# An earlier gate for casting loads, slice-wise accumulation over four tiles, and three matmuls moved ahead of a wait

## The chip, the core and the metric

The kernel runs on one core of a Trainium2 chip. The metric is the time of one execution on the device in microseconds (us), the median of several runs. A core has a tensor engine (PE, with its weight loads as PEld), a vector engine (DVE), a scalar engine (ACT), GpSimd (POOL) and a sync engine (SP), which run side by side and wait for each other by semaphores. Its transfers run on 16 DMA engines. Here the sync engine issues plain loads and stores, and GpSimd issues loads that cast float32 to bf16 on the way.

## The reference

Two matrix products with a gelu between them; a is 1024x1024, b 1024x2048, c 2048x1024, all float32.

```python
def reference(a, b, c):
    h = np.matmul(a, b)
    h = 0.5 * h * (1 + np.tanh(np.sqrt(2 / np.pi) * (h + 0.044715 * h ** 3)))
    return np.matmul(h, c).astype(np.float32)
```

## The kernel before

The kernel works in bf16, and in three stages. The first multiplies a with the left half of b (columns 0 to 1023), 16 output tiles of 128x512, by plain accumulation over eight slices k of the contraction. The second does the right half of b, the third the product with c, both with a scheme of seven block products instead of eight (`Seven`). The change touches the first stage only.

In that stage the first half of the contraction (k = 0 to 3) comes as float32 by eight plain loads of 512 KB each, which ACT and DVE cast to bf16. The second half (k = 4 to 7), the rest of b, and c come by casting loads from GpSimd. GpSimd issues none of them before it has copied one element of a plain load into `gate`: that copy waits for the load.

```python
    def load_a(h, q):        # rows 512*h.., columns 256*q.. of a, as float32
        nc.sync.dma_start(out=sta[:, h, q], in_=av[:, 4 * h:4 * h + 4, ds(q * 256, 256)])

    def load_b(q, c):        # slices k = 2q, 2q+1 of b, columns 512*c..
        nc.sync.dma_start(out=stb[:, c, 2 * q:2 * q + 2], in_=bv[:, 2 * q:2 * q + 2, ts(c, H)])

    load_a(0, 0)             # 1
    load_b(0, 0)             # 2
    load_a(1, 0)             # 3
    load_a(0, 1)             # 4
    load_b(1, 0)             # 5
    load_a(1, 1)             # 6
    load_b(0, 1)             # 7
    load_b(1, 1)             # 8

    nc.gpsimd.tensor_copy(gate, sta[:, 1, 1, 3, 0:1])
    # ... the casting loads, all on GpSimd's queue, in this order:
    for h in (0, 1):
        for m in (0, 2):     # a, second half of the contraction: four of 256 KB (as bf16)
            st = pieces("m", 4, [128, 2, H], BF16, "a2")
            nc.gpsimd.dma_start(out=st, in_=av[:, 4 * h + m:4 * h + m + 2, ds(KH * 128, H)])
            a2[h, m] = st
    for k in range(KH, KT):  # b, left half, k = 4..7: four of 256 KB
        nc.gpsimd.dma_start(out=b1[:, k], in_=bv[:, k, 0:1024])
    # ... four of 512 KB for the right half of b, eight of 512 KB for c
```

The tensor engine takes a tile of the output in a PSUM bank and adds one slice at a time; `turn1` and `turn` transpose pieces of a with the identity matrix (eight transposes), and DVE copies the result to `aT`.

```python
    def mm1(p, t, h, ks, k0=0, k1=KT):
        for k in ks:
            nc.tensor.matmul(p, b1[:, k, ts(t, 128)], aT[:, h, k],
                             start=(k == k0), stop=(k == k1 - 1))

    def block(h, tiles, ks):
        for k in ks:
            for t in tiles:
                mm1(ps[h, t], t, h, (k,), 0, KH)

    # ...
    block(0, range(4), (0, 1))
    turn1(1, 0, 5, cast_a(1, 0, nc.vector))
    turn1(0, 1, 7, cast_a(0, 1, nc.scalar))
    for t in range(3):
        ps[1, t] = bank(4 + t)
    block(1, range(3), (0, 1))
    cast_b(2, 0)
    cast_b(3, 0)
    ab = cast_a(1, 1, nc.vector)
    block(0, range(4), (2,))
    turn1(1, 1, 7, ab)
    block(0, range(4), (3,))
    for k in range(KH):
        cast_b(k, 1)         # ACT casts loads 7 and 8
    # ...
    for t in range(4):
        leave(0, t)          # ACT (even t) and DVE (odd t) move banks to SBUF
    block(1, range(3), (2, 3))
    ps[1, 3] = bank(7)
    mm1(ps[1, 3], 3, 1, range(KH), 0, KH)
    for t in range(4):
        leave(1, t)
    # ...
    T2 = [(h, t) for h in range(2) for t in range(4, 8)]
    for n, (h, t) in enumerate(T2[:7]):       # first half of the contraction
        ps[h, t] = bank(n)
        mm1(ps[h, t], t, h, range(KH))
        if n in (2, 3, 4, 5):
            turn(n // 4, 2 * (n % 2), 7)
    one.t3()
    one.t2()
    for h, t in T2[:7]:                       # second half
        mm1(ps[h, t], t, h, range(KH, KT))
        gelu(t, h, ps[h, t])
    p = bank(7)
    mm1(p, 7, 1, range(KT))
    gelu(7, 1, p)
    # ... then the tiles moved out above, second half: banks 0 to 7 once more
```

Of the kernel before, what the change touches and what calls it, by code (L numbers as in the profile page):

```python
# [19 lines left out]
def kernel(ctx, tc, a, b, c, out):  # L20
    nc = tc.nc
# [4 lines left out]
    KT = K // 128  # L26
# [13 lines left out]
    def slot(tag, shape, dt, name):  # L40
        return big.tile(shape, dt, name=name, tag=tag)

    def bank(i, shape=(128, H), dt=F32, name="ps"):
        return pp.tile(list(shape), dt, name=name, tag=f"bank{i}", padded_shape=None)

    def pieces(tag, bufs, shape, dt, name):
        return small.tile(shape, dt, name=name, tag=tag, bufs=bufs)
# [5 lines left out]
    gate = consts.tile([128, 1], F32, name="gate")  # L53
# [9 lines left out]
    KH = KT // 2  # L63
    stb = slot("x0", [128, 2, KH, H], F32, "stb")
    sta = slot("x1", [128, 2, 2, 4, 256], F32, "sta")
# [13 lines left out]
    load_b(0, 1)  # L79
    load_b(1, 1)  # L80

    nc.gpsimd.tensor_copy(gate, sta[:, 1, 1, 3, 0:1])  # L82
    nc.scalar.activation(g, warm[:, 0:1], AF.Gelu_apprx_tanh)
    wps = bank(7, name="warmps")
    for _ in range(7):
# [18 lines left out]
    def copy(eng, dst, src):  # L104
        if eng is nc.scalar:
            nc.scalar.activation(dst, src, AF.Copy)
        else:
            nc.vector.tensor_copy(dst, src)
# [6 lines that stand above are left out]
    def gelu(t, h, p):  # L115
        nc.scalar.activation(hT[h][:, t], p, AF.Gelu_apprx_tanh)  # L116

    ps = {(0, t): bank(t) for t in range(4)}
# [7 lines left out]
    def cast_a(h, q, eng):  # L126
        ab = pieces("ab", 2, [128, 4, 256], BF16, "ab")
        copy(eng, ab, sta[:, h, q])
        return ab

    def turn1(h, q, i, ab):
        pt = bank(i, (128, 2, H), BF16, "pt")
        for n in range(2):
            for m in range(4):
                nc.tensor.transpose(pt[:, n, ts(m, 128)], ab[:, m, ts(n, 128)], ident)
        nc.vector.tensor_copy(aT[:, h, 2 * q:2 * q + 2], pt)

    def cast_b(k, c, n=1):
        for i in range(n):
            r = ds(i * (H // n), H // n)  # L140
            nc.scalar.activation(b1[:, k, ds(c * H + i * (H // n), H // n)], stb[:, c, k, r], AF.Copy)  # L141
# [5 lines that stand above are left out]
# [5 lines left out]
    cast_b(1, 0)  # L152
    block(0, range(4), (0, 1))
    turn1(1, 0, 5, cast_a(1, 0, nc.vector))
    turn1(0, 1, 7, cast_a(0, 1, nc.scalar))
    for t in range(3):
        ps[1, t] = bank(4 + t)
    block(1, range(3), (0, 1))
    cast_b(2, 0)
    cast_b(3, 0)  # L160
    ab = cast_a(1, 1, nc.vector)
# [88 lines left out]
    T2 = [(h, t) for h in range(2) for t in range(4, 8)]  # L250
# [4 lines left out]
            turn(n // 4, 2 * (n % 2), 7)  # L255
    one.t3()
    one.t2()
    for h, t in T2[:7]:
        mm1(ps[h, t], t, h, range(KH, KT))
        gelu(t, h, ps[h, t])  # L260
    p = bank(7)
    mm1(p, 7, 1, range(KT))
# [3 lines left out]
    for n in range(8):  # L266
        h, t = divmod(n, 4)
# [156 lines left out]
```

## Time and profile before

| | |
|---|---|
| time, median of 3 runs | 122.31 us (122.23 to 122.33) |
| span of the profiled execution | 120.5 us |
| PE busy | 112.4 us, 93% |
| DVE, ACT, POOL busy | 88.4, 53.3, 14.6 us |
| loads landing: first, sixth, eighth plain load | 4.5, 12.6, 15.3 us |
| granted clock of PE | 0.993 |

Times in the profile count from the start of the span. A line of the timeline names the start, the length, the engine, the line of the kernel (L112 is the matmul in `mm1`, L135 the transposes of `turn1`, L108 and L106 copies and casts on DVE and ACT, L141 ACT's casts of b, L82 the gate), and in brackets how long the engine had been idle and what ended that. A busy matmul is drawn with its way through the array, so it overlaps the next one; how fast a stream runs is read from the starts. The landing times above are those at which the first reader of a load began.

### The profile page before, as it was taken

Reading aid. Unit: us, or ns where it says so; the run is one execution under the profiler, and the core shown is the slowest. Engines: PE = TensorE matmul, PEld = TensorE weight load, DVE = VectorE, ACT = ScalarE, POOL = GpSimd, SP = SyncE. Lnnn points to the kernel's source line nnn. Section 1 sums busy time; section 2 is a strip of 40 time slices with the busy share of each in tenths; the row PEclk is TensorE's granted clock in tenths of the full one; section 3 lists DMA queues with packets and bytes.
Section 4 is the critical chain, followed back from the end, with each engine's and each line's share of the span. In section 5 each row is a group of like instructions: output and inputs, shape, how many; then the busy total and the mean of one; then the engine's idle time right before and its main releaser. Section 6 shows DMA issues by size and latency. Waiting matters only on the chain.

```text
span 120.5 us, 1459 instructions
## 1 busy us (share of the span) xinstructions
PE 112.4 (93%) x550; PEld 72.7 (60%) x550; DVE 88.4 (73%) x92; ACT 53.3 (44%) x86; POOL 14.6 (12%) x27
## 2 busy tenths in 40 slices
PE   6985999969999999999999999999999999999970
PEld 2633545624444444888888444468888888888850
DVE  0243589488017899978779999979999996892490
ACT  4046490005637779946669636900012595100000
POOL 2000895462322000000000000000000000000000
PEclk9999999999999999999999999999999999999997
DMA  2999999999999999997000000062000002004695
GB/s 85 283 371 367 305 167 202 168 205 207 207 207 213 212 212 209 212 212 145 1 5 0 5 0 0 0 250 98 0 0 0 5 0 87 0 0 174 235 352 197
DMA packets 11463, 16.86 MB, mean 140 GB/s; under 512 B 705, under 2 KB 5825, under 8 KB 11457
## 3 DMA queue, kind: packets, MB, share of 16 engines
q0 software_dynamic: 5952, 8.39, 40.1%
q1 hardware_dynamic: 5504, 8.39, 19.8%
q8 instruction: 4, 0.07, 0.2%
q14 instruction: 3, 0.02, 0.1%
HBM read 20.97 MB, written 4.19 MB: 209 GB/s over the span
## 4 chain that ended last, share of the span: by engine, by line
PE 62%; DMA 21%; DVE 6%; POOL 4%; SPq 2%; issue 1%; ACT 1%; DVEq 0%; ACTq 0%
PE ps L239 50%; PE ps L112 12%; DMA b<-in_b_dram 8%; DMA sta<-in_a_dram 8%; DMA out_dram<-ot 5%; DVE x L197 4%; POOL a L93 2%; DVE ot L285 2%; POOL b L96 1%; SPq L68 1%; SPq L71 1%; DVE ot L370 1%; ACT u L280 1%; POOL gate L82 0%; DVEq L285 0%
## 5 line engine op out<-in xcount | busy, mean ns | idle before, releaser
L112 PE MATMUL ps<-aT,b 128*128 128x512 bf16 x128 | 29.2, 379 | 1.7 <-DMA b<-in_b_dram 1.2
L239 PE MATMUL ps<-x,s 128*128 128x512 f32 x128 | 29.6, 391 | 0.0
L239 PEld LDWEIGHTS ps<-x,s 128*128 128x128 f32 x128 | 24.0, 188 | 5.1
L112 PEld LDWEIGHTS <-b 128*128 128x128 bf16 x128 | 12.1, 98 | 15.9 <-DMA b<-in_b_dram 2.0
L239 PE MATMUL ps<-x,x 128*128 128x512 f32 x64 | 14.8, 389 | 0.0
L239 PE MATMUL ps<-c_sb,hT 128*128 128x512 bf16 x64 | 14.0, 379 | 0.0
L239 PEld LDWEIGHTS ps<-x,x 128*128 128x128 f32 x64 | 12.0, 188 | 2.5
L280 ACT ACTIVATE v<-ps 128x512 f32<-128x512 f32 x8 | 4.8, 599 | 17.1 <-PE ps L239 17.1
L116 ACT ACTIVATE hT<-ps 128x512 bf16<-128x512 f32 x12 | 6.8, 595 | 12.1 <-PE ps L112 12.1
L239 PE MATMUL ps<-x 128*128 128x512 f32 x48 | 11.3, 393 | 0.0
L239 PEld LDWEIGHTS <-hT 128*128 128x128 bf16 x64 | 6.2, 97 | 7.6 <-issue 0.3
L270 DVE TENSOR_TENSOR half<-ps,half 128x512 f32<-128x512 f32 x8 | 5.5, 692 | 7.0 <-PE ps L112 6.6
L239 PEld LDWEIGHTS ps<-x 128*128 128x128 f32 x48 | 9.0, 188 | 2.0
L197 DVE TENSOR_TENSOR x<-c_sb 128x1024 fp32r<-128x1024 bf16 x8 | 9.2, 1215 | 0.0
L285 DVE TENSOR_TENSOR ot<-ps,v 128x512 f32<-128x512 f32 x8 | 5.3, 687 | 4.6 <-DMA out_dram<-ot 3.8
L141 ACT ACTIVATE b<-stb 128x512 bf16<-128x512 f32 (+1 forms) x9 | 4.7, 573 | 6.6 <-DMA stb<-in_b_dram 6.6
L285 DVE TENSOR_TENSOR ot<-ps,u 128x512 f32<-128x512 f32 x8 | 5.4, 691 | 3.0 <-ACT u L280 3.0
L116 ACT ACTIVATE hT<-ot 128x512 bf16<-128x512 f32 x12 | 7.0, 624 | 1.2 <-DVE ot L285 1.2
L239 PE MATMUL ps<-aT,b 128*128 128x512 bf16 x32 | 7.1, 379 | 0.0
L102 POOL DMA_DIRECT2D c_sb<-in_c_dram x8 | 5.7, 712 | 8.9 <-DMA b<-in_b_dram 8.9
L280 ACT ACTIVATE p<-ps 128x512 f32<-128x512 f32 x8 | 4.6, 594 | 4.8 <-PE ps L239 4.8
L116 ACT ACTIVATE hT<-half 128x512 bf16<-128x512 f32 x8 | 5.0, 631 | 2.6 <-DVE half L270 2.6
(47 smaller groups left out, 114.7 us busy)
## 6 DMA issues: line engine op xcount, KB each, us to landing
c_sb<-in_c_dram POOLq DMA_DIRECT2D x8, 512.0 KB, 20.2
out_dram<-ot SPq DMA_DIRECT2D x16, 256.0 KB, 2.1
sta<-in_a_dram SPq DMA_DIRECT2D x4, 512.0 KB, 6.9
stb<-in_b_dram SPq DMA_DIRECT2D x4, 512.0 KB, 8.9
b<-in_b_dram POOLq DMA_DIRECT2D x4, 512.0 KB, 13.8
a<-in_a_dram POOLq DMA_DIRECT2D x4, 256.0 KB, 5.6
b<-in_b_dram POOLq DMA_DIRECT2D x4, 256.0 KB, 8.9
```

Source lines behind the costliest of these rows:

```text
L68: nc.sync.dma_start(out=sta[:, h, q], in_=av[:, 4 * h:4 * h + 4, ds(q * 256, 256)])
L71: nc.sync.dma_start(out=stb[:, c, 2 * q:2 * q + 2], in_=bv[:, 2 * q:2 * q + 2, ts(c, H)])
L93: nc.gpsimd.dma_start(out=st, in_=av[:, 4 * h + m:4 * h + m + 2, ds(KH * 128, H)])
L102: nc.gpsimd.dma_start(out=c_sb[:, t:t + 2], in_=cv[:, t:t + 2])
L112: nc.tensor.matmul(p, b1[:, k, ts(t, 128)], aT[:, h, k], start=(k == k0), stop=(k == k1 - 1))
L116: nc.scalar.activation(hT[h][:, t], p, AF.Gelu_apprx_tanh)
L141: nc.scalar.activation(b1[:, k, ds(c * H + i * (H // n), H // n)], stb[:, c, k, r], AF.Copy)
L197: nc.vector.tensor_tensor(out=dst[:, r], in0=x[:, r], in1=y[:, r], op=op)
L239: nc.tensor.matmul(p[:, ds(c0, w)], l[:, k, ts(j, 128)], r[:, k, ds(c0, w)], start=(start and k == 0), stop=(k == self.kt - 1), skip_group ...
L270: nc.vector.tensor_tensor(out=half[:, h, t], in0=p, in1=half[:, h, t], op=ADD)
L280: nc.scalar.activation(st, p, AF.Copy)
L285: nc.vector.tensor_tensor(out=ot, in0=p, in1=st, op=ADD)
```

## The change

It has three parts, all in the first stage. The gate copies an element of the fifth plain load instead of the sixth, so that GpSimd issues the casting loads earlier. Three of the six matmuls of the block for the lower rows of a (slice k = 0) are put ahead of the transposes of the fourth plain load, to stand where the tensor engine waits for that load's cast. And the second half of the contraction over the first four of the tiles in `T2` goes slice by slice over all four, instead of tile by tile, so that a slice of b is needed later than before. Nothing is computed otherwise, and the number of instructions is the same.

```diff
-    nc.gpsimd.tensor_copy(gate, sta[:, 1, 1, 3, 0:1])
+    nc.gpsimd.tensor_copy(gate, stb[:, 0, 3, 0:1])
...
     turn1(1, 0, 5, cast_a(1, 0, nc.vector))
-    turn1(0, 1, 7, cast_a(0, 1, nc.scalar))
     for t in range(3):
         ps[1, t] = bank(4 + t)
-    block(1, range(3), (0, 1))
+    ab = cast_a(0, 1, nc.scalar)
+    block(1, range(3), (0,))
+    turn1(0, 1, 7, ab)
+    block(1, range(3), (1,))
...
-    for h, t in T2[:7]:
-        mm1(ps[h, t], t, h, range(KH, KT))
+    for k in range(KH, KT):
+        for h, t in T2[:4]:
+            mm1(ps[h, t], t, h, (k,))
+    for n, (h, t) in enumerate(T2[:7]):
+        if n >= 4:
+            mm1(ps[h, t], t, h, range(KH, KT))
         gelu(t, h, ps[h, t])
```

## The prediction

> **What bounds the kernel now.** I read the page first, then the chain that ended last, the waits, the timeline up to 48 us, and short windows for the DMA traffic. From the page's third and fourth parts and the chain in order of time (start us, length us, what):
>
> ```profile
> PE 62%; DMA 21%; DVE 6%; POOL 4%; SPq 2%; issue 1%; ACT 1%; DVEq 0%; ACTq 0%
> ```
>
> ```profile
> 3.48 9.11 DMA sta<-in_a_dram
> ...
> 12.64 0.18 POOL gate L82
> 12.82 2.92 POOL a L93 x4
> 15.74 1.57 POOL b L96 x3
> 17.32 9.97 DMA b<-in_b_dram
> ...
> 27.33 14.20 PE ps L112 x65
> 41.53 60.69 PE ps L239 x272
> ```
>
> From 27.33 us on the tensor engine decides. I looked for starts of its matmuls over 0.3 us apart after that time and found only two (0.42 us each, at 48 and 80 us). So whatever moves the 27.33 moves the end, one for one. Before 27.33 the chain runs through the gate: the sixth load lands, GpSimd opens the gate, issues eight casting loads, and the last slice of b (k=7) ends a wait of the tensor engine. The chain looks as if an earlier gate would pay in full. Two other views say that it can't.
>
> The timeline (start us, length us, engine, line, operation, idle before):
>
> ```profile
> 9.00 0.62 PE L135 MATMUL pt<-ident,ab 128*128 128x128 bf16 x8
> ...
> 10.93 0.62 PE L135 MATMUL pt<-ident,ab 128*128 128x128 bf16 x8 [1.31 <-ACT ab L106]
> ...
> 12.68 0.69 DVE L108 CAST ab<-sta 128x1024 bf16<-128x1024 f32 x1 [0.40 <-DMA sta<-in_a_dram]
> ...
> 13.99 5.85 PE L112 MATMUL ps<-aT,b 128*128 128x512 bf16 x26
> ...
> 15.27 1.15 ACT L141 ACTIVATE b<-stb 128x512 bf16<-128x512 f32 x2 [0.15 <-DMA stb<-in_b_dram]
> ...
> 16.32 2.04 ACT L106 ACTIVATE half<-ps 128x512 f32<-128x512 f32 x4
> ```
>
> ```profile
> 24.30 1.46 PE L112 MATMUL ps<-aT,b 128*128 128x512 bf16 x6
> ...
> 26.09 0.39 PE L112 MATMUL ps<-aT,b 128*128 128x512 bf16 x1 [0.34 <-DMA b<-in_b_dram]
> ...
> 27.33 14.20 PE L112 MATMUL ps<-aT,b 128*128 128x512 bf16 x65 [0.85 <-DMA b<-in_b_dram]
> ```
>
> One matmul of 512 columns takes (14.20-0.38)/64 = 0.216 us from start to start. The six at 24.30 are four of tile 6 and k=4, k=5 of the first tile; that tile's k=6 and k=7 then wait for their slices. Without waits k=7 would have started at 24.30+7x0.216 = 25.81; it started at 27.33. So **1.52 us** is really lost, more than the 1.2 us in the table of waits, since a busy matmul is drawn 0.38 us long.
>
> The windows of one microsecond (the last three columns are clock, DMA share, GB/s):
>
> ```profile
> 13.00:14.00 1.00, 1.00 (x13) 0.64 (x11) 0.38 (x1) 0.04 (x1) 1.00 (x2) 1.00 1.04 383
> 14.00:15.00 1.00, 1.00 (x8) 0.45 (x6) 0.80 (x2) 1.00 (x2) 1.00 (x2) 1.00 0.88 156
> 15.00:16.00 1.00, 1.00 (x6) 0.42 (x5) 1.00 (x2) 0.85 (x3) 1.00 (x3) 1.00 1.06 135
> ```
>
> The eight plain loads run the DMA engines full until 14. The casting loads replace them: the trace's packets by queue have the first casting packet at 14.43, 1.8 us after the gate's copy at 12.64, and the plain queue's last data at 14.8. The rate is counted in bytes written, half of those read where a load casts, so about 207 (28 to 31 us) is a casting load's full rate; at 15 to 16 the queue is still starting.
>
> **What the Trainium skill says.** "DMA: Bandwidth & Descriptors", section "Queues, rings and completion order", says that each DMA engine round-robins between the queues it has work for. So two queues that both have work share, and neither is free for the other. This trace shows almost no overlap of the two (14.4 to 14.8), so it neither confirms nor denies it. The same page, "Latency and other measured facts", gives about 1 us to the first byte on the GpSimd path; here it was 1.8 us from the gate's copy, of which the first issue is 0.74. "TensorE: Matmul & The Clock Gate", section "Back-to-back issue gap", gives some 216 ns for an isolated 512-column matmul and 131 in a stream; here 216 is the spacing in the stream too, and 131 is not reached. "PSUM — Partial Sum Buffer", section "The four PSUM rules", lets accumulation groups in different banks interleave, since a group's start clears its own bank only; so going slice by slice costs no extra instruction. The trace of before has it in the first block (four banks, k outermost) at the same 0.216 us.
>
> **The change part by part.** No instruction is added or removed.
>
> *Slice by slice.* With k outermost over four tiles, k=4 of four tiles comes first (0.86 us), then k=5, and so on: k=6 is needed 8x0.216 = 1.73 us after the start of this part, k=7 2.59 us after it. The part starts at 24.30+4x0.216 = 25.16, so they are needed at 26.89 and 27.75. They landed at 26.09 and 27.33. Even with unchanged landings both waits go, with 0.4 us to spare: **-1.52 us**. The four gelus then come together; ScalarE needs 0.60 each, 2.4 us, against 12 matmuls of tiles 4 to 6 (2.6 us) and the eight of the last tile before the first bank is used again. No new wait.
>
> *Three matmuls ahead.* The tensor engine waits from 9.6 to 10.93 for ScalarE's cast of the fourth piece of a. Three matmuls of tile row 1 (0.65 us) now stand there: they need the transposed piece that VectorE finished copying at 10.35, so they run 10.4 to 11.05, and the transposes start some 0.1 us later than now. That removes 0.65 us of work from after the wait, but the next stop swallows it: the transposes at 13.55 need VectorE's cast of the sixth load, 12.68+0.69 = 13.37, which landed at 12.6 either way. They can come from 13.55 to 13.43 and no further: **-0.12 us**.
>
> *The gate.* It waits for the fifth load, not the sixth. ScalarE's cast of that load (the trace's timeline has it at 11.13) puts its landing near 11.1, so the gate opens some 1.5 us sooner, at 11.15, and casting packets start at about 14.43-1.5 = 12.95. The sixth load's data is through by then (12.07 in the packets). The seventh has half a microsecond left, the eighth all of its 1.35: the plain queue has about 1.4 us of work left (mean over the 16 engines), of which 1.25 after the slower first casting packets. From there it shares. If the shares are equal, each 2 KB plain packet (2048 B x16/385 GB/s = 85 ns) is followed by a casting packet (1024 B x16/207 GB/s = 79 ns), and the last plain load comes 1.25x79/85 = 1.2 us later. If the casting queue starts as slowly as it did (25, 59, 72 packets in the first half microseconds against a steady 100), some 135 of them come in between: 135/16x79 ns = 0.7 us. I take **d = 1.0**.
>
> Who waits for the eighth load? ScalarE casts it at 15.27, in two (1.15 us), then moves the first bank out (0.58, from 16.32 to 16.90); the first of the 12 matmuls on the right half of b waits for both. It started at 17.09 (13.99+14x0.216, and 0.08 of a hiccup), so there was 0.13 us of slack on ScalarE's side after the semaphore. With the 0.12 of the reordering the tensor engine would come there at 16.97, just when ScalarE is done. So all of d becomes a new wait on the tensor engine: **+d = +1.0 us**. What the earlier gate brings in return, k=4 to k=7 perhaps 0.5 us sooner, is worth nothing, since slice by slice they are in time anyway.
>
> Sum: -1.52 - 0.12 + 1.0 = -0.64 us, and 122.31 - 0.64 = 121.67. I put it a little lower, **121.6 us**, since the slow start of the casting queue is what the trace shows, and equal shares are what it doesn't.
>
> **The rivals.** (1) Plain loads undisturbed: if the casting queue gets nothing while the other has work, d is 0 and the time 120.7. For it: the plain packets at 14.5 to 14.7, beside the first casting ones, took 84 to 95 ns as ever, while those casting packets took 350 to 1000. Against it: that is the tail of the queue, some 20 packets. (2) The starved plain load: the casting queue gets half or more from its first packet, and its reads are slower than steady (130 ns a packet at 15 us against 98 later). Then d is 1.6 to 2, the wait removed comes back as a wait for ScalarE's cast, and the time is 122.3 to 122.7. For it: queues share. (3) The gate pays as the chain suggests: k=7 lands 1.5 us sooner and everything follows. Against it: DMA share is about 1 from 3 us to 54 us, so the work only changes order; only the 0.3 us of idle engines and the slow start around 14.5 can be won. (4) A new wait for k=7 because the casting loads come no sooner while the tensor engine does: the 0.4 us to spare speak against it.
>
> **Range and chances.** d between 0.3 and 1.7 gives 121.0 to 122.4; I take 120.9 to 122.3. Even d = 0 is -1.3%, so faster by over 2% would need a gain that no step has; slower by 2% would need d above 4 us.
>
> **What would show it.** The table of waits of after should have no wait of the tensor engine for b's casting loads, and a new one of 0.7 to 1.2 us, near 17 us, for ScalarE's casts or its moves of the first banks; ScalarE should wait for the last stb load until 16 to 16.5 instead of 15.27. The gate's copy should stand at 11.1 to 11.2. The wait of the transposes for ScalarE's cast should shrink from 1.31 to near zero, and the transposes of the sixth load should start at 13.43. The steady part (65 matmuls at 27.33) should start 0.6 us sooner in equal count. If the eighth load still lands at 15.3, rival 1 holds; if it lands after 16.9, rival 2.

## The result, and the profile after

| | before | changed |
|---|---|---|
| median | 122.32 us (4 runs, 122.23 to 122.36) | 120.73 us (4 runs, 120.46 to 122.70) |
| ratio | | 0.9861, interval 0.9844 to 0.9878 |

By the medians the change takes off 1.59 us, 1.3%; by the ratio it is 1.7 us (1.5 to 1.9). The prediction was 121.6 with a range from 120.9 to 122.3, so the kernel is faster than its range. Its rival 1 (plain loads undisturbed) had named 120.7.

One of the four runs, at 122.70 us, was a slow one, in whose trace the tensor engine ran at half pace from 8 to 11 us; the ratio leaves it out, and the profile read here is that of the same kernel measured again (120.68 us). In this kernel the matmul of stage 1 is still L112 and the transposes of the first half L135; the second stage's matmul is L241, since lines moved by two.

The timeline of the changed kernel (start, length, engine, line, operation, idle before), to be laid beside the lines shown of before:

```profile
10.36 0.81 PE L112 MATMUL ps<-aT,b 128*128 128x512 bf16 x3 [0.78 <-DVE aT L136]
...
11.18 0.18 POOL L82 COPY gate<-stb 128x1 f32<-128x1 f32 x1 [9.87 <-DMA stb<-in_b_dram]
...
12.70 0.69 DVE L108 CAST ab<-sta 128x1024 bf16<-128x1024 f32 x1 [0.35 <-DMA sta<-in_a_dram]
...
13.45 0.62 PE L135 MATMUL pt<-ident,ab 128*128 128x128 bf16 x8
...
13.91 5.85 PE L112 MATMUL ps<-aT,b 128*128 128x512 bf16 x26
...
15.29 1.15 ACT L141 ACTIVATE b<-stb 128x512 bf16<-128x512 f32 x2 [0.16 <-DMA stb<-in_b_dram]
16.35 2.04 ACT L106 ACTIVATE half<-ps 128x512 f32<-128x512 f32 x4
...
24.21 4.48 PE L112 MATMUL ps<-aT,b 128*128 128x512 bf16 x19
```

The gate's copy stands at 11.18 instead of 12.64, so GpSimd does issue 1.46 us sooner. But the eighth plain load is read at 15.29, against 15.27 before: nothing was taken from it. The 26 matmuls begin at 13.91 instead of 13.99 and go on without a hole. From 24.21 on there is no stop for a slice of b, where before there were two, at 26.09 and 27.33. The chain shows what that is worth at the end; the second stage starts at 39.91 us instead of 41.53, 1.62 us sooner:

```profile
24.37 3.24 PE ps L112 x15
...
27.66 10.74 PE ps L112 x49
...
38.45 1.46 PE ps L112 x6
39.91 25.31 PE ps L241 x113
```

In the table of waits (waiter, releaser, us in total, times, longest) between 4 and 30 us the tensor engine's matmuls and transposes have these three, and none for a load:

```profile
PE ps L112 <- ACT b L141: 1.0, 1, 1.0
PE ps L112 <- DVE aT L136: 0.8, 1, 0.8
...
PE pt L135 <- DVE ab L108: 0.2, 1, 0.2
```

And the windows of one microsecond, with the clock, the DMA share and GB/s in the last three columns:

```profile
13.00:14.00 1.00, 0.97 (x11) 0.55 (x10) 0.39 (x1) 0.02 (x1) 1.00 (x2) 1.00 1.05 387
14.00:15.00 1.00, 1.00 (x7) 0.40 (x5) 0.89 (x2) 1.00 (x2) 1.00 (x3) 1.00 1.18 262
15.00:16.00 1.00, 1.00 (x6) 0.46 (x5) 1.00 (x2) 0.84 (x3) 1.00 (x3) 1.00 1.24 204
```

From 13 to 14 the plain loads still have their full rate, 387 GB/s, though the first casting load was issued by 12.13 (11.30, where the issue begins, and 0.83 for it). From 15 the casting loads are at full rate at once (204 against 135 before). So the earlier gate put them in line sooner, and they went when most of the plain loads were through.

### The profile page after: what moved, and what is told of

It is laid out like the page before. It is cut to its first block, busy times and chain, and to the rows that moved or that the text cites. A ratio compares the mean times of both kernels' runs of the same rounds, so it can differ in the third digit from the quotient of the medians.

```text
span 120.9 us, 1452 instructions
## 1 busy us (share of the span) xinstructions
PE 112.8 (93%) x544; PEld 72.6 (60%) x550; DVE 88.5 (73%) x92; ACT 52.8 (44%) x86; POOL 14.7 (12%) x27
## 4 chain that ended last, share of the span: by engine, by line
PE 77%; DMA 10%; DVE 7%; issue 1%; ACT 1%; SPq 0%; DVEq 0%; ACTq 0%
PE ps L241 50%; PE ps L112 24%; DMA out_dram<-ot 5%; DMA stb<-in_b_dram 5%; DVE x L199 4%; DVE ot L291 2%; PE pt L187 2%; DVE aT L136 1%; PE pt L135 1%; DVE ot L376 1%; ACT u L286 1%; SPq L68 0%; ACT b L141 0%; DVEq L291 0%; DVEq L376 0%
## 5 line engine op out<-in xcount | busy, mean ns | idle before, releaser
L112 PE MATMUL ps<-aT,b 128*128 128x512 bf16 x124 | 30.5, 395 | 2.9 <-ACT b L141 1.7
L241 PE MATMUL ps<-x,s 128*128 128x512 f32 x128 | 29.6, 391 | 0.0
L241 PEld LDWEIGHTS ps<-x,s 128*128 128x128 f32 x128 | 24.0, 188 | 5.1
L112 PEld LDWEIGHTS <-b 128*128 128x128 bf16 x128 | 12.5, 100 | 17.4 <-issue 2.9
L241 PE MATMUL ps<-x,x 128*128 128x512 f32 x64 | 14.8, 389 | 0.0
L241 PE MATMUL ps<-c_sb,hT 128*128 128x512 bf16 x62 | 13.9, 379 | 0.1
L241 PEld LDWEIGHTS ps<-x,x 128*128 128x128 f32 x64 | 12.0, 188 | 2.5
L116 ACT ACTIVATE hT<-ps 128x512 bf16<-128x512 f32 x12 | 6.3, 602 | 12.4 <-PE ps L112 12.4
L241 PE MATMUL ps<-x 128*128 128x512 f32 x48 | 11.3, 394 | 0.0
L241 PEld LDWEIGHTS <-hT 128*128 128x128 bf16 x64 | 6.2, 98 | 7.6 <-issue 0.3
L241 PEld LDWEIGHTS ps<-x 128*128 128x128 f32 x48 | 9.0, 188 | 2.0
L241 PE MATMUL ps<-aT,b 128*128 128x512 bf16 x32 | 7.1, 379 | 0.0
L136 DVE COPY aT<-pt 128x1024 bf16<-128x1024 bf16 x4 | 2.8, 692 | 5.1 <-PE pt L135 5.1
```

Of the source, the lines that this page charges most:

```text
L112: nc.tensor.matmul(p, b1[:, k, ts(t, 128)], aT[:, h, k], start=(k == k0), stop=(k == k1 - 1))
L241: nc.tensor.matmul(p[:, ds(c0, w)], l[:, k, ts(j, 128)], r[:, k, ds(c0, w)], start=(start and k == 0), stop=(k == self.kt - 1), skip_group ...
```

## The experiments

Each kernel was timed beside the kernel before on the same chip, whose median was 122.4 to 122.5 us. A time is the median of four runs or more, except where one run is named. "Landing", "read at" and the first packets are those of one trace of each kernel.

**The changed kernel once more**, for the trace shown above; the kernel is the same.

> The changed kernel once more, for a trace whose tensor clock is full: 120.5 to 120.8 us. Theory A (plain loads undisturbed: while the plain queue has work the casting queue takes next to nothing from it): the eighth plain load is read by ScalarE at 15.2 to 15.4 us, as before, and no wait of the tensor engine at 17 us. Theory B (the queues do share, but the casting queue starts some 2 us after its gate and slowly, so it meets only the plain queue's tail): the eighth load at 15.4 to 15.8. Theory C (the load is late by my 1 us, and something else made up for it): 16 us or later.

Measured: 120.82 us, ScalarE reads the eighth load at 15.29, and the twelve matmuls on the right half of b run without a wait. Theory C falls. The 15.29 is in A's range, but it does not tell A's rule from a late start as in B, since the first casting packet came only at 14.00, 2.8 us after the gate's copy.

**The gate back at the sixth load, the rest of the change kept.**

```diff
-    nc.gpsimd.tensor_copy(gate, stb[:, 0, 3, 0:1])
+    nc.gpsimd.tensor_copy(gate, sta[:, 1, 1, 3, 0:1])
```

> The changed kernel with the gate back at the sixth load. If the slices alone take the waits away, as the prediction has it (k=6 needed at 26.9, k=7 at 27.7, landed at 26.1 and 27.3): 120.7 us, the same as the changed kernel within 0.2 us, under theories A and B. Under theory C it is faster than the changed kernel by up to 1 us. If the gate is what brought the gain: 121.5 or more, with waits for the casting loads of b on the tensor engine.

Measured: 120.70 us (120.53 to 120.86), beside 120.82 (120.51 to 121.72) with the gate at the fifth load on the same chip. In the changed kernel no gain from the earlier gate shows within this spread.

**The slices alone**, and **the three matmuls alone**, each in the kernel before.

```diff
-    for h, t in T2[:7]:
-        mm1(ps[h, t], t, h, range(KH, KT))
+    for k in range(KH, KT):
+        for h, t in T2[:4]:
+            mm1(ps[h, t], t, h, (k,))
+    for n, (h, t) in enumerate(T2[:7]):
+        if n >= 4:
+            mm1(ps[h, t], t, h, range(KH, KT))
         gelu(t, h, ps[h, t])
```

> The kernel before with the slices alone. The prediction's step: both waits for k=6 and k=7 go, 1.52 us less, 120.8 us, and no wait of the tensor engine for the casting loads of b. If the gain needs the earlier gate: 121.3 us or more and a wait left. The spread between chips and runs is 0.2 us.

Measured: 120.83 us, ratio 0.9864 (0.9850 to 0.9879). That is 1.7 us, the whole of the change within the interval (1.5 to 1.8 us). The timeline of this kernel has 20 matmuls in one piece, and GpSimd's issue that waits for the k=7 slice at 27.33 (in the kernel before such an issue, at 27.57, follows 0.24 us after the matmul on that slice); the tensor engine doesn't need that slice before 24.17+16x0.216 = 27.62:

```profile
24.17 4.70 PE L112 MATMUL ps<-aT,b 128*128 128x512 bf16 x20
...
27.33 0.72 POOL L102 DMA_DIRECT2D c_sb<-in_c_dram  x1 [0.52 <-DMA b<-in_b_dram]
```

```diff
-    turn1(0, 1, 7, cast_a(0, 1, nc.scalar))
     for t in range(3):
         ps[1, t] = bank(4 + t)
-    block(1, range(3), (0, 1))
+    ab = cast_a(0, 1, nc.scalar)
+    block(1, range(3), (0,))
+    turn1(0, 1, 7, ab)
+    block(1, range(3), (1,))
```

> The kernel before with the three matmuls moved alone. The prediction's step: 0.12 us before the transposes of the sixth load, and then nothing at the end, because the wait for k=7 stays where its load puts it: 122.3 us, within 0.2 us of the kernel before. If the order matters by itself: 121.7 or less.

Measured: 122.37 us, ratio 0.9990 (0.9981 to 0.9998), so 0.12 us (0.02 to 0.23). The waits for the slices are all still there, and a little longer than before: in this trace the tensor engine arrives 0.07 us sooner (24.23), and the k=7 slice lands 0.22 us later:

```profile
26.23 0.39 PE L112 MATMUL ps<-aT,b 128*128 128x512 bf16 x1 [0.55 <-DMA b<-in_b_dram]
...
27.55 1.25 PE L112 MATMUL ps<-aT,b 128*128 128x512 bf16 x5 [0.93 <-DMA b<-in_b_dram]
```

**The gate at the fifth load alone**, in the kernel before.

```diff
-    nc.gpsimd.tensor_copy(gate, sta[:, 1, 1, 3, 0:1])
+    nc.gpsimd.tensor_copy(gate, stb[:, 0, 3, 0:1])
```

> The kernel before with the gate at the fifth load alone. The tensor engine still wants k=6 and k=7 at 25.6 and 25.8 us. If they land 0.3 to 0.5 us sooner, as the prediction has it, 121.8 to 122.0 us; if they land 1.5 us sooner, as the chain of the kernel before suggests, 120.8 to 121.0 us; with the eighth load late by 1 us, 122.3 or more. Theory A and B: between 121.0 and 122.0 us.

Measured: 121.32 us, by the medians 1.1 us less than the kernel before; the ratio is uncertain (0.9851, 0.9782 to 0.9920). In the trace the k=6 wait is gone, and k=7 starts at 26.41 instead of 27.33, 0.92 us sooner:

```profile
24.36 1.67 PE L112 MATMUL ps<-aT,b 128*128 128x512 bf16 x7
...
26.41 2.33 PE L112 MATMUL ps<-aT,b 128*128 128x512 bf16 x9 [0.37 <-DMA b<-in_b_dram]
```

Without waits k=7 would have started at 24.36+7x0.216 = 25.87, so 0.54 of the 1.52 us lost before remain. By medians and trace the earlier gate is worth about 1 us where nothing else removes the waits, and nothing that shows where the slices do. The gains of the two parts overlap; they don't add up.

**The gate at the third, the first, and the fourth load**, in the changed kernel: how much do the plain loads suffer from casting loads that are issued in the middle of them?

```diff
-    nc.gpsimd.tensor_copy(gate, stb[:, 0, 3, 0:1])
+    nc.gpsimd.tensor_copy(gate, sta[:, 1, 0, 3, 0:1])   # third load
+    nc.gpsimd.tensor_copy(gate, sta[:, 0, 0, 3, 0:1])   # or the first
+    nc.gpsimd.tensor_copy(gate, sta[:, 0, 1, 3, 0:1])   # or the fourth
```

> The changed kernel with the gate at the third load (lands at 8.2 us), so that casting packets can start at about 10 us with more than 4 us of plain loads to go. Theory A: the eighth load still lands at 15.3 us, time 120.5 to 120.8. Theory B: equal shares delay the sixth to the eighth load by 1.5 to 4 us, ScalarE reads the eighth at 17 to 19 us, and the time is 122.3 to 124.5 us.

Measured: 122.00 us, outside what A allows and just under what B gave. The issue begins at 8.77, and the first casting packet comes at 13.12. The eighth load is read at 16.41, and the tensor engine stops for ScalarE's move of the first bank, as the prediction had drawn it for the gate at the fifth load:

```profile
8.77 2.99 POOL L93 DMA_DIRECT2D a<-in_a_dram  x4
...
16.41 1.15 ACT L141 ACTIVATE b<-stb 128x512 bf16<-128x512 f32 x2 [1.46 <-DMA stb<-in_b_dram]
...
17.47 2.04 ACT L106 ACTIVATE half<-ps 128x512 f32<-128x512 f32 x4
...
18.10 2.75 PE L112 MATMUL ps<-aT,b 128*128 128x512 bf16 x12 [0.94 <-ACT half L106]
```

That wait of 0.94 us is drawn short by the way through the array; the start is 18.10 against 17.0 in the changed kernel, 1.1 us, and 1.2 to 1.3 is what the time lost.

> The changed kernel with the gate at the first load (lands near 4.4 us). With the gate at the third load the first casting packet came 4.3 us after its issue, at 13.0 us, and from there the two queues moved packets one for one. Theory P (the casting packets queue up behind a fixed number of plain packets that the DMA engines have already taken in, some 3.3 us of them): first casting packet at 8 to 9.5 us, then one for one, the sixth to the eighth plain load late by 2 us and more, eighth read by ScalarE after 17.5 us, time 123 to 126 us. Theory Q (the plain queue goes first until its last load or two, whenever the casting loads are issued): first casting packet at 13 us again, eighth load read at 16.0 to 16.7 us, time 121.7 to 122.3 us as with the gate at the third load.

Measured: 127.68 us. The first casting packet came at 9.40, again 4.4 us after the issue began, and from then on the two queues moved packets one for one: in the trace's packets 110 casting and 103 plain between 10 and 11 us, 116 and 125 in the next, 117 and 123, 119 and 124. Theory P's packets are there, and Q falls; the time is above the 126 us that P allowed. The plain loads pay for it; the sixth is read at 16.28 instead of 12.7, the seventh at 18.97, the eighth at 22.33:

```profile
16.28 0.69 DVE L108 CAST ab<-sta 128x1024 bf16<-128x1024 f32 x1 [3.73 <-DMA sta<-in_a_dram]
...
18.97 1.15 ACT L141 ACTIVATE b<-stb 128x512 bf16<-128x512 f32 x2 [5.73 <-DMA stb<-in_b_dram]
...
22.33 1.15 ACT L141 ACTIVATE b<-stb 128x512 bf16<-128x512 f32 x2 [2.21 <-DMA stb<-in_b_dram]
```

> The changed kernel with the gate at the fourth load (lands at 9.8 us). Theory P, now with its number (a casting packet waits behind up to about 60 plain packets per DMA engine that were there first; 68 were left with the gate at the third load, 27 at the fifth): here some 45 to 50 are left when the first casting load has been issued, near 10.8 us, so all of them go first, the first casting packet comes at 13.8 to 14.1 us, the eighth load is read at 15.2 to 15.4 us, and the time is 120.5 to 120.9. Against it, if the two queues share by some other rule once the casting packets have waited 2 to 3 us: first casting packet at 13 us or before, eighth load at 15.6 to 16.4, time 121.0 to 122.0.

Measured: 120.94 us, the first casting packet at 13.77, the eighth load read at 15.51:

```profile
9.82 2.99 POOL L93 DMA_DIRECT2D a<-in_a_dram  x4
...
15.51 1.15 ACT L141 ACTIVATE b<-stb 128x512 bf16<-128x512 f32 x2 [0.48 <-DMA stb<-in_b_dram]
```

Nearly all of the plain packets went first. The eighth load is some 0.3 us late (this run was 0.08 ahead of the other at the fourth load), a little more than theory P allowed.

**The gate at the eighth load**, a single run, to measure how long a casting load takes with no other in its way.

```diff
-    nc.gpsimd.tensor_copy(gate, stb[:, 0, 3, 0:1])
+    nc.gpsimd.tensor_copy(gate, stb[:, 1, 3, 0:1])
```

> The changed kernel with the gate at the eighth load, so that no plain packet is left when the casting loads are issued: this measures how long a casting load takes by itself from the gate's copy to its first packet. Theory P: 1.0 to 1.8 us (in the kernel before it was 1.8 with 9 plain packets per engine left). The slices then wait for the casting loads, 122 us or more.

Measured: 123.33 us. Copy at 15.26, the first load issued from 15.38 to 16.21, its first packet at 16.92: 1.66 us from the copy, 0.71 from the end of the issue, with no plain packet left. Here the slices do wait:

```profile
15.26 0.18 POOL L82 COPY gate<-stb 128x1 f32<-128x1 f32 x1 [13.95 <-DMA stb<-in_b_dram]
...
27.74 1.04 PE L112 MATMUL ps<-aT,b 128*128 128x512 bf16 x4 [0.56 <-DMA b<-in_b_dram]
```

The six places of the gate together, from the trace's DMA packets by queue. All but one row are the changed kernel with its gate moved. The third column counts plain packets not yet done 0.71 us after the end of the first casting load's issue, when its packets could have come; the fourth how many of them were done when the sixteenth casting packet started. Both are totals divided by the 16 DMA engines, since the trace doesn't name a packet's engine.

| gate at load | first packet after the copy, us | plain packets left | of these went first | eighth load read at, us | time, us |
|---|---|---|---|---|---|
| 8th | 1.66 | 0 | 0 | 15.22 | 123.33 |
| 6th (kernel before) | 1.79 | 1.8 | 1.8 | 15.27 | 122.31 |
| 6th | 1.65 | 0.6 | 0.6 | 15.48 | 120.70 |
| 5th (the change) | 2.82 | 18.6 | 16.7 | 15.29 | 120.82 |
| 4th | 4.07 | 35 | 33 | 15.51 | 120.94 |
| 3rd | 5.00 | 56 | 45 | 16.41 | 122.00 |
| 1st | 5.01 | 128 | 58 | 22.33 | 127.68 |

In the second row for the sixth load the whole trace runs late, with the second load read at 6.98 us instead of 6.71 for the gate at the fifth, so its 15.48 is not the gate's doing. In the last two rows the gate's copy itself took 0.70 us instead of 0.18.

A casting packet goes behind the plain packets that were there before it, up to some 45 to 58 per engine. The plain packets beyond that alternate with the casting ones. With the third load the mean hides two kinds of engines: by the packets that signal the end of a load, seven ended their part of the eighth load by 14.67, nine between 15.03 and 16.03. The 45 and the 58 are one amount in bytes: the plain packets are of 1 KB for a and of 2 KB for b, and those that went first add up to 67 and 68 KB per engine in the last two rows. Both took 3.0 us to go. So the limit may be an amount of data or a time; as the plain loads ran at one rate in both, these runs don't tell the two apart, nor what holds the plain packets ahead.

**A version meant to beat both**: the cast of the sixth load split between VectorE and ScalarE, and the first bank moved out by VectorE.

```diff
-    ab = cast_a(1, 1, nc.vector)
+    ab = pieces("ab", 2, [128, 4, 256], BF16, "ab")
+    copy(nc.vector, ab[:, 0:2], sta[:, 1, 1, 0:2])
+    copy(nc.scalar, ab[:, 2:4], sta[:, 1, 1, 2:4])
...
-        copy(nc.vector if t % 2 else nc.scalar, half[:, h, t], ps[h, t])
+        dve = t % 2 or (h, t) == (0, 0)
+        copy(nc.vector if dve else nc.scalar, half[:, h, t], ps[h, t])
```

> The changed kernel, with the cast of the sixth load split between VectorE and ScalarE and the first bank moved out by VectorE instead of ScalarE. In the changed kernel the tensor engine waits at 13.45 us for that cast and at 14.85 us for the copy after it, and the right half of b starts at 17.0 us with ScalarE done at 16.9. If those three are the next limit: the transposes at 13.3, the right half of b at 16.6 to 16.8 us, and 0.2 to 0.4 us less than the changed kernel, 120.3 to 120.5 us. If the eighth load is the limit all the same: the changed kernel's time within 0.1 us.

Measured: 120.55 us, on another chip than the changed kernel's runs so far. Both were then run five times on one chip.

> The changed kernel beside the next one on the same chip, 120.5 to 120.9 us.

> The changed kernel with the cast of the sixth load split and the first bank moved out by VectorE: 0.2 to 0.35 us less than the changed kernel on the same chip if the earlier run (120.55 us) holds; the same within 0.1 us if that was the chip.

Measured: the changed kernel 120.73 us (120.61 to 120.77), this version 120.55 (120.52 to 120.82). The medians are 0.18 us apart, a little under the 0.2 to 0.35 expected, but the runs overlap, and so do the ratios to before (0.9858, 0.9834 to 0.9882; and 0.9854, 0.9831 to 0.9876). A gain is not shown. In the traced one of these runs the second plain load was read late:

```profile
6.98 1.24 ACT L141 ACTIVATE b<-stb 128x256 bf16<-128x256 f32 x3 [4.75 <-DMA stb<-in_b_dram]
...
13.56 0.61 PE L135 MATMUL pt<-ident,ab 128*128 128x128 bf16 x8
...
14.01 5.85 PE L112 MATMUL ps<-aT,b 128*128 128x512 bf16 x26
```

That read stood anywhere from 6.51 to 6.98 us in the traces (7.34 in that of the 122.70 us run), and what follows moves with it where the gate leaves the plain loads alone: the eighth load was read at 15.13 where it was 6.51 (the slices alone), and at 15.52 here. That spread is larger than the 0.18 us between the medians.

## Why the prediction was wrong

*The bound.* Right. Behind the slices the tensor engine decides: the second stage starts 1.62 us sooner in the chain, and the time is 1.59 us less by the medians, 1.7 by the ratio.

*Slice by slice.* Right, with its size: -1.52 predicted, -1.7 (1.5 to 1.8) alone. The needed times held too, since k=7 landed before 27.62 with the gate at the sixth load, and no wait came up.

*Three matmuls ahead.* Right. The wait for ScalarE's cast is gone (0.78 us for VectorE's copy stands there, before the three matmuls), the transposes of the sixth load moved from 13.55 to 13.45 (13.43 predicted), held by VectorE's cast, and by itself the move is worth 0.02 to 0.23 us at the end.

*The gate.* Here the step failed. The prediction said that "casting packets start at about 14.43-1.5 = 12.95", and took d = 1.0 us from it as the delay of the eighth load. The gate's copy came where it was expected (11.15; 11.18), but the first casting packet at 14.00: 18.6 plain packets per engine were there before it and all but 1.9 of them went first. So the eighth load hardly paid: d is 0.02 us by the traces (15.27 and 15.29), and no wait came up at 17 us. Put d = 0 into the sum and it gives -1.64 us and 120.67; measured were -1.59 and 120.73. The 1.8 us from copy to packet had been read as the way's own length and carried over; its own length is 1.66, and the packet's place in line comes on top.

*What the earlier gate brings in return.* "Worth nothing" was right: with the gate back at the sixth load the time is the same within the runs' spread. The k=7 slice did come sooner, which is seen from GpSimd's issue behind it, here before and after:

```profile
27.57 0.72 POOL L102 DMA_DIRECT2D c_sb<-in_c_dram  x1 [0.52 <-DMA b<-in_b_dram]
```

```profile
26.37 0.71 POOL L102 DMA_DIRECT2D c_sb<-in_c_dram  x1 [0.51 <-DMA b<-in_b_dram]
```

That is 1.2 us and not the 0.5 of the prediction: the first casting packet came 0.43 us sooner, and from 15 to 19 us 800 casting packets ended instead of 667. The gate alone, without slices, turns that into about 1 us.

*The rivals.* Rival 1 had the number, but as a rule ("gets nothing while the other has work") it is wrong: with the gate at the third or first load the casting queue gets its share while plain packets wait. Rival 2 is in part what happens there (122.00 and 127.68 us): the casting queue gets half, though its reads are not slower, 96 ns a packet. Rival 3, the gate paying as the chain suggests, holds in part for the kernel before. Rival 4, a new wait for k=7, did not come. The sign in the trace that the prediction named for rival 1, plain packets of 84 to 95 ns beside casting packets that took 350 to 1000, pointed to the right number by luck. With the gate at the eighth load, where no plain packet is left, the first eight casting packets take 414 to 598 ns all the same; with it at the fifth, behind plain packets, they take 96 to 98. So the slow packets go with a casting queue that starts with no plain packets ahead of it, and say nothing of who goes first.

*Sharing.* Round robin between queues that have work, as the Trainium skill has it ("DMA: Bandwidth & Descriptors", section "Queues, rings and completion order"), agrees with the packets of the gate at the first load, 110 to 103. The sentence doesn't tell when a queue gets its first turn, and the prediction read it as if it did.

## What to carry to other kernels

Two changes that remove the same wait are not a sum: ask of each what it is worth with the other in place, and here, once reordering let the data be needed later, fetching it sooner brought nothing that shows. A load's delay from issue to first packet, read where the queue in front was nearly empty, can't be carried to where it isn't; count the packets that are ahead. Issuing a second stream of loads a little before the first one ended cost the first nothing here (0.02 us) and saved the second its slow start, while issuing it far before, with more than about 67 KB of plain data per engine ahead, gave it every other packet at the cost of the loads that were needed first.

## What was not expected of the hardware

The wait behind plain packets already in line, up to 67 or 68 KB per engine or 3.0 us, and the one-for-one sharing after it (110 to 103 packets in a microsecond). And the start of the casting loads: issued when the plain queue was nearly through they ran at 135 GB/s from 15 to 16 us; issued 1.5 us sooner, and kept waiting for 1.2 us more than with an empty queue, they ran at 204 in the same microsecond. With the gate at the eighth load and no plain packet left they started as slowly, 73 packets in their first microsecond and 139 in the next, against 113 and 198 with the gate at the fifth. That the wait gives the queue time to fill is an explanation that no run tests.
